# Six norms of an encoder trunk: the spread of rsqrt by a DRAM round trip in place of diagonals and a matmul with ones

## The chip, the cores and the metric

The kernel runs on one NeuronCore of one Trainium2 chip. The core has a tensor engine (PE, with its weight loads shown apart as PEld), a vector engine (DVE), a scalar engine (ACT), GpSimd (POOL) and SyncE (SP), which issues most of the DMA transfers. Each engine works through its own instructions in the order in which they were laid down, and waits on semaphores for the others. The metric is the device time of one execution in microseconds, and less is better.

## The reference

The model is a trunk of two layers over 1024 tokens of width 1024. Layer 0 mixes tokens with grouped-query attention, layer 1 with a chunked gMLP; both are followed by a squared-ReLU MLP. Ahead of each of these four stages stands an RMS norm that is modulated by the conditioning vector:

```python
def rmsnorm(x, g):
    xf = x.astype(jnp.float32)
    y = xf * lax.rsqrt(jnp.mean(xf * xf, axis=-1, keepdims=True) + EPS)
    return (y * g).astype(x.dtype)
...
        h = modulate(rmsnorm(x, norm1_g[i]), sh1, sc1)
...
            y = gqa_attention(h, w_qkv[j], q_g[j], k_g[j], w_o[j], cos, sin)   # layer 0
            y = chunked_gmlp(h, w_in[j], b_in[j], ...)                         # layer 1
        x = x + g1[:, None, :] * y
        h = modulate(rmsnorm(x, norm2_g[i]), sh2, sc2)
        x = x + g2[:, None, :] * sq_relu_mlp(h, mlp_w_in[i], mlp_w_out[i])
```

Everything is float32. Four norms, each over two halves of the tokens, make eight norms in the kernel.

## The kernel before

**Layout.** The activations lie transposed: the 1024 features are 8 tiles of 128 partitions, and the 1024 tokens are two halves of 512 columns. A tile `x[hf][k]` is 128 x 512. A float32 product is made of three matmuls: each operand is split into a high part (a cast on ACT, L328 in `split`) and a low part (a subtraction, L329, on DVE as a rule).

**The products.** The large products follow a Winograd/Strassen scheme with seven products ("1265473") of combinations of quarter operands. One step of it, here called a unit, is 12 matmuls of 128 x 512. `winograd` (L469 to L471 are its matmuls) makes the first product of the two MLPs and a part of gMLP's; `wino_v` makes gMLP's other part; `Out` (L1212 to L1214) makes the products that come back to width 1024. Each of these calls a hook after a unit, with the unit's number, and the hook traces the work of the next norm between the products.

**The norm.** `SquareSum` adds up the squares of 8 tiles as they become final. `norm_ss` then sums over the 128 partitions with four small matmuls against a column of ones (L274), which leaves the mean square of token p + 128 j at partition p and column j. DVE adds EPS and scales (L276), and POOL raises this to the power of -0.5 (L242, in `rsqrt_small`), which gives `r`, 128 x 4. But the activations need it with tokens along the columns and the same value on all partitions. So ACT makes four diagonals, the identity times a column of r (L284; L280 does it in one DVE instruction for the first two norms), and `norm_rb` multiplies them by a matrix of ones (L289): every partition of the 128 x 512 result holds the 512 values. The result is read from PSUM (`keep`) or copied to SBUF by ACT first (L293).

**Its use.** `norm_h` multiplies a tile by rb (L334) and applies scale and shift (L335). `forms_a` makes the eight such tiles of half 0 and splits them, one tile a step; `more` takes steps from its list. `forms_b` makes the eight tiles of half 1 and the combinations "6", "5", "4", "7", "3" that the scheme needs (L376, L377, L388); its list has four steps for the tiles with "6", then one for each other combination. The first units use half 0 alone: with FIRST = 6 the MLPs' first twelve units are "1" and "2", and "6" is first wanted by unit 12; `wino_v` wants it at unit 8.

**The places.** Two norms (layer 0, ahead of attention) are not touched. The other six, numbered as they come:

1. Layer 0, second norm, half 0: in the loop over the output projection (L1425 to L1431). `norm_ss` after block m = 0, `norm_rb` and the first steps after m = 1. A block is 24 matmuls.
2. Layer 0, second norm, half 1: in `mlp`'s hook `at`, at unit HB[0] = 2; `norm_rb` and `forms_b` at HB + HR = 4, then one step a unit.
3. Layer 1, first norm, half 0: `norm_hook`, called over the last 32 units of MLP 0's output; `norm_ss` at m = HK = 3, `norm_rb` at m = 5, then a step at every odd m.
4. Layer 1, first norm, half 1: in `gmlp`'s hook, at unit HBV = 1; `norm_rb` at 3, then steps at 4 to 7, 10, 12, 16 and 20.
5. Layer 1, second norm, half 0: `norm_hook` again, over the last 24 units of gMLP's output.
6. Layer 1, second norm, half 1: as number 2, with HB[1] = 1 and HR[1] = 1, so at unit 1 and unit 2.

**Order.** The code is traced as written, and a scheduler lays the instructions of each engine in an order of its own: among those that are ready by its own estimate of time, the one that was traced first goes first. `pin` keeps an instruction behind the one traced before it on its engine; `hold` does so in the first stage alone. Tiles come from pools: `slot()` takes one of 58 SBUF tiles "t" of 128 x 512, `bank_x` and `bank_y` one of four PSUM banks each. The `dram` pool holds what is kept in DRAM between stages.

Of the kernel before, what the change touches and what calls it, by code (L numbers as in the profile page):

```python
# [11 lines left out]
F32 = mybir.dt.float32  # L12
F32R = mybir.dt.float32r
AF = mybir.ActivationFunctionType
ALU = mybir.AluOpType
# [3 lines left out]
P = 128  # L19
D = 1024  # L20
# [16 lines left out]
def encoder_kernel(ctx: ExitStack, tc: tile.TileContext, t: dict, out: bass.AP):  # L37
# [3 lines left out]
    const = ctx.enter_context(tc.tile_pool(name="const", bufs=1))  # L41
    small = ctx.enter_context(tc.tile_pool(name="small", bufs=3))
    mem = ctx.enter_context(tc.tile_pool(name="mem", bufs=1))

    uid = [0]

    def nm(s):
        uid[0] += 1
        return f"{s}_{uid[0]}"
# [220 lines left out]
    def norm_ss(sqs, bank, wide_dg=False):  # L270
        acc = sqs.acc
        ps = bank("ss")[:, :4]
        for j in range(4):
            hold(T.matmul(ps[:, j : j + 1], acc[:, j * P : (j + 1) * P], ones[:, 0:1], start=True, stop=True))  # L274
        ms = small.tile([P, 4], F32, tag="ms", name=nm("ms"))
        hold(V.tensor_scalar(ms, ps, 1.0 / D, EPS, ALU.mult, ALU.add))  # L276
        r = rsqrt_small(ms, 4)
        dg = slot()
        if wide_dg:
            hold(V.tensor_tensor(dg.rearrange("p (j q) -> p j q", j=4), ident.unsqueeze(1).broadcast_to([P, 4, P]),  # L280
                                 r.unsqueeze(2).broadcast_to([P, 4, P]), ALU.mult))
            return dg
        for j in range(4):
            S.activation(dg[:, j * P : (j + 1) * P], ident, AF.Copy, scale=r[:, j : j + 1])  # L284
        return dg

    def norm_rb(dg, bank, keep=False):
        ps = bank("rb")
        hold(T.matmul(ps, ones, dg, start=True, stop=True))  # L289
        if keep:  # L290
            return ps
        rb = slot()
        S.copy(rb, ps)  # L293
        return rb

    def norm_u(xk, layer, which, k, rb):
# [42 lines left out]
    def forms_a(xt, layer, which, rb):  # L339

        f = {"raw": {}}

        def step(k):
            if k < KT:
                f["raw"][k] = norm_h(xt[k], layer, which, k, rb, G if k in NA else V)
            if k:
                f[("1" if k < 5 else "2", (k - 1) % 4)] = split(f["raw"][k - 1])

        f["todo"] = [lambda k=k: step(k) for k in range(KT + 1)]
        return f  # L350
# [742 lines left out]

    es_a.close()
    p_y = ctx.enter_context(tc.tile_pool(name="p_y", bufs=4, space=PSUM))
    dram = ctx.enter_context(tc.tile_pool(name="dram", bufs=1, space=bass.MemoryType.DRAM))

    class Out:


# [239 lines left out]
    def mlp(layer, fs, sqs, done, hook):  # L1340
        hidden = forms_dram(16)
        out_ = Out(t["wm"][layer], hidden, 4, mod[:, layer, 5])
        quad = {}
        f = {}
        stores = []

        def sink(c, m, hf):
            S.activation(c, c, AF.Relu)
            S.activation(c, c, AF.Square)
            p = m // 2  # L1350
            quad[(m, hf)] = c
            q = early((m % 2, hf))
            if q:
                nc.scalar.dma_start(hidden[p][q], c)
                if q == "1" and p < FIRST:
                    del quad[(m, hf)]
                elif q == "2" and p < FIRST:
                    quad[(m - 1, 0)] = slot()
                    nc.sync.dma_start(quad[(m - 1, 0)], hidden[p]["1"])
            else:  # L1360
                tiles = {(j, h): quad.pop((m + j, h)) for j in range(2) for h in range(2)}
                stores.extend(spread(tiles, hidden[p], slot, V))

        n = 16 * 7
        rest = []
        halves = None if layer else Halves(late)

        def at(i):
            more(f, RW, None)
            if halves:  # L1370
                h = i - 13
                if 0 <= h < 2 * KT:
                    spill(h // KT, (h % KT,))
                elif h == 2 * KT:
                    halves.start()
                elif h == 2 * KT + 4:
                    halves.silu()
                    halves.load()
                    halves.load()
                elif h > 2 * KT + 6 and h % MX == 0:  # L1380
                    halves.step()
            if i == HB[layer]:
                rest.append(norm_ss(sqs[0], bank_y))
            elif i == HB[layer] + HR[layer]:
                rest[:] = forms_b(f, x[1], layer, 1, norm_rb(rest[0], bank_y, True), "5473")
            elif i > HB[layer] + HR[layer] and rest:
                rest.pop(0)()
            if stores and i % 7 > 0 and i % 7 != 6:
                stores.pop(0)()
            out_.ahead(i - n)  # L1390

        yield from winograd(lambda m: t["wi"][layer, m], 16, f, sink, FIRST, at, lambda: (cut(8), f.update(fs[0])))

        def at_out(i):
            if stores and i > 2:
                stores.pop(0)()
            if i == CUT:
                cut(4)
            if halves and i in XL:
                load_xs(*XL[i])  # L1400
            if hook and i >= out_.n - out_.tail:
                hook(i - out_.n + out_.tail)

        if halves:
            load_xs(*XL[-1])
        out_.run(at_out, done)
# [13 lines left out]
    for m in range(WA):  # L1420
        if m == WA - 1:
            mlp0_fs, mlp0_sqs = [None], [sqB]
            mlp0.append(mlp(0, mlp0_fs, mlp0_sqs, lambda *a: add_sq(*a), lambda i: hook0(i)))
            next(mlp0[0])
        wo_mm(m, (1,), bank_y)  # L1425
        if m == 0:
            fA = norm_ss(sqA, bank_x)
        elif m == 1:
            fA = forms_a(x[0], 0, 1, norm_rb(fA, bank_x))
        if m:  # L1430
            more(fA, RQ, None)  # L1431
    cond.clear()

# [6 lines left out]
    def norm_hook(layer, which, bank):  # L1440
        dg = []

        def hook(m):
            if m == HK:
                dg.append(norm_ss(sq[0], bank))
                sq[0] = SquareSum()
            elif m == HK + 2:
                fg.append(forms_a(x[0], layer, which, norm_rb(dg[0], bank)))
                more(fg[-1], 1, None)
            elif m > HK + 2:  # L1450
                more(fg[-1], m % 2, None)
        return hook

# [156 lines left out]
    def gmlp(f, sqB, done, hook):  # L1610
        rest = []

        def at(i):
            more(f, RW, None)
            if i == HBV:
                spill(0)
                rest.append(norm_ss(sqB, bank_y))
            elif i == HBV + 2:
                rest[:] = forms_b(f, x[1], 1, 0, norm_rb(rest[0], bank_y), "5734", True)
            elif rest and i in (*range(HBV + 3, HBV + 7), 10, 12, 16, 20):  # L1620
                rest.pop(0)()
                if len(rest) == 4:
                    spill(1)
# [147 lines left out]
HK = 3  # L1771
# [79 lines left out]
```

## Time and profile before

| | us |
|---|---|
| Median of the runs shown (3) | 2627.94 |
| Lowest and highest of them | 2626.04, 2629.11 |
| Profiled execution, span from first to last instruction | 2625.8 |

The profile gives no time of that execution beside its span; the median of the runs lies 2.1 us above it.

| Engine | busy us | share of the span | instructions |
|---|---|---|---|
| PE | 2601.6 | 99% | 12860 |
| DVE | 2183.1 | 83% | 3276 |
| ACT | 1451.1 | 55% | 2612 |
| POOL | 723.2 | 28% | 531 |

The profile is of one execution. A row of a group gives the line, the engine, the operation, output and inputs by the program's names, the shapes and the count, then busy time and the mean duration in ns, then the idle time of the engine ahead of it and what ended that. A row of a timeline gives start and duration in us, the engine, the line, and in brackets the idle time before and what ended it. A row of a window gives its length, then busy time and count for PE, PEld, DVE, ACT and POOL, the granted PE clock, the DMA engines' busy share and GB/s. Matmuls are pipelined: a duration of 0.39 us overlaps the next one, and the distance between starts is what a matmul costs. Tiles are named by their pool's tag, so many tiles are called t.

### The profile page before, as it was taken

How to read it: one execution, taken by the hardware profiler on the slowest of the kernel's cores; microseconds unless marked ns; L12 is line 12 of the kernel's file. 1: busy time of each engine (PE TensorE's matmuls, PEld its weight loads, DVE VectorE, ACT ScalarE, POOL GpSimd, SP SyncE). 2: the span in 40 equal slices, each digit the busy share in tenths (PEclk: the TensorE clock that was granted, in tenths of full speed). 3: DMA queues.
4: the chain of work that ended last, by engine and by line, in shares of the span. 5: the costliest groups of instructions: out<-in, count | busy, mean ns of one | idle time of the engine just before them, and what ended most of it. 6: DMA issues, size and time to landing. Idle time of an engine off the chain costs nothing. (4 is left out here: it accounts for less than half of the span.)

```text
span 2625.8 us, 37307 instructions
## 1 busy us (share of the span) xinstructions
PE 2601.6 (99%) x12860; PEld 2172.2 (83%) x12860; DVE 2183.1 (83%) x3276; ACT 1451.1 (55%) x2612; POOL 723.2 (28%) x531
## 2 busy tenths in 40 slices
PE   9999999999999999999999999999999999999999
PEld 7789999888788888888888888888888788888887
DVE  7868999887989989877897687788979977789974
ACT  4569999854654455446543354445456645465442
POOL 0238776533000004430122054451520000005400
PEclk9999999999999999999999999999999999999999
DMA  8010222234486788545243355568641554487461
GB/s 306 27 33 9 74 88 75 97 112 145 168 288 245 270 310 306 192 133 172 82 136 121 120 174 175 178 204 305 237 141 50 177 179 156 153 310 268 149 211 58
DMA packets 208752, 435.39 MB, mean 166 GB/s; under 512 B 23025, under 2 KB 35441, under 8 KB 208562
## 3 DMA queue, kind: packets, MB, share of 16 engines
q1 hardware_dynamic: 181682, 395.24, 44.7%
q10 hardware_dynamic: 26880, 37.76, 4.0%
q8 instruction: 102, 1.67, 0.3%
q14 instruction: 88, 0.72, 0.1%
HBM read 310.23 MB, written 122.68 MB: 165 GB/s over the span
## 5 line engine op out<-in xcount | busy, mean ns | idle before, releaser
L1212 PE MATMUL out<-t,s 128*128 128x512 f32 x1232 | 479.9, 390 | 0.9 <-ACT t L328 0.8
L1213 PE MATMUL out<-t,s 128*128 128x512 f32 x1232 | 479.3, 389 | 0.7 <-DVE t L329 0.7
L1214 PE MATMUL out<-t,s 128*128 128x512 f32 x1232 | 478.9, 389 | 0.0
L469 PE MATMUL w<-t,s 128*128 128x512 f32 x1168 | 459.8, 395 | 0.9 <-ACT t L328 0.5
L470 PE MATMUL w<-t,s 128*128 128x512 f32 x1168 | 455.2, 390 | 1.8 <-DVE t L329 1.8
L471 PE MATMUL w<-t,s 128*128 128x512 f32 x1168 | 454.7, 389 | 0.0
L329 DVE TENSOR_TENSOR t<-t,t 128x512 fp32r<-128x512 f32 x408 | 324.7, 806 | 36.2 <-ACT t L328 29.0
L328 ACT CAST t<-t 128x512 fp32r<-128x512 f32 x408 | 245.3, 617 | 122.2 <-DMA t<-hf 71.7
L1213 PEld LDWEIGHTS out<-t,s 128*128 128x128 f32 x1232 | 231.2, 188 | 50.2 <-DVE t L329 1.8
L1212 PEld LDWEIGHTS out<-t,s 128*128 128x128 f32 x1232 | 231.2, 188 | 50.2 <-ACT t L328 1.7
L1214 PEld LDWEIGHTS out<-t,s 128*128 128x128 f32 x1232 | 231.2, 188 | 48.1
L454 ACT CAST s<-w 128x512 fp32r<-128x512 f32 x292 | 173.4, 616 | 161.4 <-PE w L471 104.3
L470 PEld LDWEIGHTS w<-t,s 128*128 128x128 f32 x1168 | 219.3, 188 | 49.7 <-DVE t L329 5.2
L469 PEld LDWEIGHTS w<-t,s 128*128 128x128 f32 x1168 | 219.3, 188 | 49.4 <-issue 2.9
L471 PEld LDWEIGHTS w<-t,s 128*128 128x128 f32 x1168 | 219.2, 188 | 45.6
L455 DVE TENSOR_TENSOR s<-w,s 128x512 fp32r<-128x512 f32 x292 | 221.8, 766 | 41.1 <-ACT s L454 40.6
L1194 ACT CAST s<-t 128x512 fp32r<-128x512 f32 x240 | 148.2, 620 | 187.0 <-PE out L1214 136.3
L1180 POOL TENSOR_TENSOR w<-w,t 128x512 f32<-128x512 f32 x20 | 34.2, 1721 | 767.7 <-DMA t<-hf 691.5
L1195 DVE TENSOR_TENSOR s<-t,s 128x512 fp32r<-128x512 f32 x240 | 195.1, 814 | 56.1 <-ACT s L1194 55.4
L951 DVE TENSOR_REDUCE mx<-s 128x1 f32<-128x1024 f32 x128 | 156.2, 1220 | 30.5 <-PE s L948 29.2
L974 DVE TENSOR_TENSOR t<-t,t 128x512 fp32r<-128x512 f32 x256 | 164.1, 681 | 17.1 <-ACT t L968 16.4
L984 PE MATMUL o<-t,t 128*128 128x256 f32 x1024 | 162.6, 291 | 0.0
(251 smaller groups left out, 5089.1 us busy)
## 6 DMA issues: line engine op xcount, KB each, us to landing
t<-hf SPq DMA_DIRECT2D x320, 256.0 KB, 4.0
hf<-c SPq DMA_DIRECT2D x156, 256.0 KB, 3.4
w<-in_wi_dram SPq DMA_DIRECT2D x64, 512.0 KB, 4.5
hf<-c ACTq DMA_DIRECT2D x96, 256.0 KB, 2.7
w<-in_ada_dram SPq DMA_DIRECT2D x36, 512.0 KB, 3.9
x<-in_ada_dram SPq DMA_DIRECT2D x64, 256.0 KB, 5.4
t<-in_wm_dram SPq DMA_DIRECT2D x64, 256.0 KB, 4.7
wf<-w SPq DMA_DIRECT2D x64, 256.0 KB, 3.0
```

Of the source, the lines that this page charges most:

```text
L328: S.copy(hi, src)
L329: (eng or V).tensor_tensor(lo, src, f32(hi), ALU.subtract)
L454: S.copy(hi, src)
L455: V.tensor_tensor(lo, src, f32(hi), ALU.subtract)
L469: T.matmul(ps, hi[:, a], th, start=kt == 0, stop=False)
L470: T.matmul(ps, hi[:, a], tl, start=False, stop=False)
L471: T.matmul(ps, lo[:, a], th, start=False, stop=kt == 3)
L974: pin(V.tensor_tensor(lo, pt, f32(hi), ALU.subtract))
L1195: V.tensor_tensor(lo, src, f32(hi), ALU.subtract)
L1212: T.matmul(ps, hi[:, a], th, start=begin and kt == 0, stop=False, **g)
L1213: T.matmul(ps, hi[:, a], tl, start=False, stop=False, **g)
L1214: T.matmul(ps, lo[:, a], th, start=False, stop=end and kt == 3, **g)
```

## The change

A new function `norm_bc` takes the place of `norm_ss` and `norm_rb` at the six places. The partition sums, the scaling and the power stay. Then `r` (128 x 4) is stored to a 4 x 128 tile in DRAM, so that the 512 values lie in the order of the tokens, and this row is loaded into all 128 partitions of an SBUF tile. Both transfers are issued by SP. The first multiplication by rb is traced three units after `norm_bc` in the hooks of half 1 (before: two, one and two units after, at places 2, 6 and 4), four units after it in `norm_hook` (before: two), and two blocks after it in the output projection (before: one). The lists of steps follow from there. The DRAM pool is opened at the start.

```diff
+    dram = ctx.enter_context(tc.tile_pool(name="dram", bufs=1, space=bass.MemoryType.DRAM))
...
+    def norm_bc(sqs, bank):
+        acc = sqs.acc
+        ps = bank("ss")[:, :4]
+        for j in range(4):
+            T.matmul(ps[:, j : j + 1], acc[:, j * P : (j + 1) * P], ones[:, 0:1], start=True, stop=True)
+        ms = small.tile([P, 4], F32, tag="ms", name=nm("ms"))
+        V.tensor_scalar(ms, ps, 1.0 / D, EPS, ALU.mult, ALU.add)
+        r = rsqrt_small(ms, 4)
+        d = dram.tile([4, P], F32, name=nm("rd"))
+        nc.sync.dma_start(d.rearrange("j p -> p j"), r)
+        rb = slot()
+        nc.sync.dma_start(rb, d.rearrange("j p -> (j p)").unsqueeze(0).broadcast_to([P, 512]))
         return rb
...
             if i == HB[layer]:
-                rest.append(norm_ss(sqs[0], bank_y))
-            elif i == HB[layer] + HR[layer]:
-                rest[:] = forms_b(f, x[1], layer, 1, norm_rb(rest[0], bank_y, True), "5473")
-            elif i > HB[layer] + HR[layer] and rest:
+                rest.append(norm_bc(sqs[0], bank_y))
+            elif i == HB[layer] + 3:
+                rest[:] = forms_b(f, x[1], layer, 1, rest[0], "5473")
+            elif i > HB[layer] + 3 and rest:
                 rest.pop(0)()
...
         if m == 0:
-            fA = norm_ss(sqA, bank_x)
-        elif m == 1:
-            fA = forms_a(x[0], 0, 1, norm_rb(fA, bank_x))
-        if m:
+            fA = norm_bc(sqA, bank_x)
+        elif m == 2:
+            fA = forms_a(x[0], 0, 1, fA)
+        if m > 1:
             more(fA, RQ, None)
...
             if m == HK:
-                dg.append(norm_ss(sq[0], bank))
+                dg.append(norm_bc(sq[0], bank))
                 sq[0] = SquareSum()
-            elif m == HK + 2:
-                fg.append(forms_a(x[0], layer, which, norm_rb(dg[0], bank)))
+            elif m == HK + 4:
+                fg.append(forms_a(x[0], layer, which, dg[0]))
                 more(fg[-1], 1, None)
-            elif m > HK + 2:
+            elif m > HK + 4:
                 more(fg[-1], m % 2, None)
...
-                rest.append(norm_ss(sqB, bank_y))
-            elif i == HBV + 2:
-                rest[:] = forms_b(f, x[1], 1, 0, norm_rb(rest[0], bank_y), "5734", True)
-            elif rest and i in (*range(HBV + 3, HBV + 7), 10, 12, 16, 20):
+                rest.append(norm_bc(sqB, bank_y))
+            elif i == HBV + 3:
+                rest[:] = forms_b(f, x[1], 1, 0, rest[0], "5734", True)
+            elif rest and i in (*range(HBV + 4, HBV + 8), 10, 12, 16, 20):
                 rest.pop(0)()
```

More of the change, by code (lines that the diff above doesn't have):

```diff
@@ L293, in norm_rb @@
         S.copy(rb, ps)
+        return rb
+    def norm_bc(sqs, bank):
[10 more added lines that the diff above has]
+        nc.sync.dma_start(rb, d.rearrange("j p -> (j p)").unsqueeze(0).broadcast_to([P, 512]))
         return rb
```

1 line of the change is left out of this document (removed).

## The prediction

> **What bounds the kernel now.** I read the page first (span, busy shares), then the groups by line for what is removed, then windows, waits and timelines around the six places.
>
> ```profile
> span 2625.8 us, 37307 instructions
> PE 2601.6 (99%) x12860; PEld 2172.2 (83%) x12860; DVE 2183.1 (83%) x3276; ACT 1451.1 (55%) x2612; POOL 723.2 (28%) x531
> L289 PE MATMUL rb<-t,ones 128*128 128x512 f32 x16 | 8.4, 606 | 1.0 <-DVE t L280 0.9 <-ACT t L284 0.2
> ```
>
> PE is busy 99% of the span: what is taken from PE's stream comes off the time, if PE isn't made to wait instead. The third row is the matmul with ones: 8 norms, each in two passes (x16), 8.4 us in all. Six of the eight go. I number them: 1 is the half 0 norm inside the output projection, 2 the half 1 norm at the start of MLP 0, 3 the half 0 norm in the tail of MLP 0's output, 4 the half 1 norm in gMLP's first product, 5 the half 0 norm in the tail of gMLP's output, 6 the half 1 norm at the start of MLP 1.
>
> What one matmul really costs is read from the starts on PE around it (number 3; the columns are start, duration, engine):
>
> ```profile
> 1190.01 0.39 PE L1214 MATMUL out<-t,s 128*128 128x512 f32 x1
> 1190.24 1.02 PE L289 MATMUL rb<-t,ones 128*128 128x512 f32 x2
> 1190.70 0.80 PE L1212 MATMUL out<-t,s 128*128 128x512 f32 x1
> 1191.34 0.40 PE L1213 MATMUL out<-t,s 128*128 128x512 f32 x1
> 1191.57 0.40 PE L1214 MATMUL out<-t,s 128*128 128x512 f32 x1
> ```
>
> The product's matmuls start 0.23 us apart (1191.34 to 1191.57). From 1190.01 the third one after would start at 1190.70 without L289; it starts at 1191.57: 0.87 us.
>
> But PE doesn't set the pace everywhere. At 2 and 6 the half 1 forms are made by VectorE in a rush, and PE waits for them (windows: length, then busy time of PE, PEld, DVE, ACT, POOL; then PE's waits in 640 to 700 and 2008 to 2060):
>
> ```profile
> 626.00:655.00 29.00, 29.00 (x131) 23.59 (x131) 28.87 (x39) 19.20 (x32) 7.44 (x3) 1.00 0.32 109
> 655.60:658.70 3.10, 2.93 (x14) 1.96 (x12) 0.16 (x2) 1.91 (x6) 1.01 (x1) 1.00 0.00 0
> 659.00:691.00 32.00, 29.68 (x120) 21.45 (x118) 31.74 (x54) 24.99 (x44) 0.00 (x0) 1.00 0.29 99
> 2019.00:2046.00 27.00, 25.23 (x108) 19.58 (x106) 26.93 (x46) 21.07 (x36) 0.00 (x0) 1.00 0.20 68
> PE w L470 <- DVE t L329: 1.8, 6, 0.5
> PE w L469 <- ACT t L328: 1.2, 1, 1.2
> ```
>
> DVE is busy 31.74 of 32 us and 26.93 of 27 us behind the two norms, PE only 29.68 and 25.23. So there the end is set by when DVE gets the spread rsqrt, plus a fixed amount of DVE work. Just ahead of 2 DVE has a hole (0.16 of 3.10 us busy): it waits for the norm. There the change is decided.
>
> **Removed.** 24 diagonals on ACT, six matmuls, four copies of rb on ACT (2 and 6 read it from PSUM). ACT is busy 55% of the span, so its share costs nothing by itself. The chain at 2:
>
> ```profile
> 655.75 1.01 POOL L242 TENSOR_TENSOR r<-ms,mhalf 128x4 f32<-128x4 f32 x1 [19.06 <-DVE ms L276]
> 656.79 1.28 ACT L284 ACTIVATE t<-ident,r 128x128 f32<-128x128 f32 x4 [2.62 <-POOL r L242]
> 657.57 0.39 PE L471 MATMUL w<-t,t 128*128 128x512 f32 x1
> 658.12 1.12 PE L289 MATMUL rb<-t,ones 128*128 128x512 f32 x2 [0.17 <-ACT t L284]
> 658.61 0.69 DVE L329 TENSOR_TENSOR t<-t,t 128x512 fp32r<-128x512 f32 x1 [2.94 <-ACT t L328]
> 659.28 0.69 DVE L334 TENSOR_TENSOR t<-x,rb 128x512 f32<-128x512 f32 x1
> 659.31 0.40 PE L470 MATMUL w<-t,t 128*128 128x512 f32 x1
> ```
>
> The diagonals stand at the head of ACT's queue for 2.62 us until POOL has r; a split (L328) waits behind them, and DVE's L329 behind that. This block goes, so DVE does that 0.6 us of work inside the hole. PE loses 659.31 - 657.57 - 2 x 0.23 = 1.28 us here, and about 0.9 us at each other place.
>
> I call c the time from r's end to the first multiply with rb (L334). The starts of L242 and L334 at the other five, in the order 1, 3, 4, 5, 6:
>
> ```profile
> 616.29 1.48 POOL L242 TENSOR_TENSOR r<-ms,mhalf 128x4 f32<-128x4 f32 x1
> 623.19 1.28 DVE L334 TENSOR_TENSOR t<-x,t 128x512 f32<-128x512 f32 x2
> 1185.07 1.44 POOL L242 TENSOR_TENSOR r<-ms,mhalf 128x4 f32<-128x4 f32 x1 [7.28 <-DVE ms L276]
> 1191.92 0.69 DVE L334 TENSOR_TENSOR t<-x,t 128x512 f32<-128x512 f32 x1
> 1269.01 1.40 POOL L242 TENSOR_TENSOR r<-ms,mhalf 128x4 f32<-128x4 f32 x1 [4.73 <-DVE ms L276]
> 1275.97 1.28 DVE L334 TENSOR_TENSOR t<-x,t 128x512 f32<-128x512 f32 x2
> 1951.58 1.43 POOL L242 TENSOR_TENSOR r<-ms,mhalf 128x4 f32<-128x4 f32 x1 [7.27 <-DVE ms L276]
> 1958.42 0.69 DVE L334 TENSOR_TENSOR t<-x,t 128x512 f32<-128x512 f32 x1
> 2014.28 1.01 POOL L242 TENSOR_TENSOR r<-ms,mhalf 128x4 f32<-128x4 f32 x1 [27.64 <-DVE ms L276]
> 2019.08 0.68 DVE L334 TENSOR_TENSOR t<-x,rb 128x512 f32<-128x512 f32 x1
> ```
>
> So c is now 5.4 at 1, 2.5 at 2 (659.28 - 656.76), 5.4 at 3, 5.6 at 4, 5.4 at 5 and 3.8 at 6.
>
> **Added.** Two transfers in a row on SP: r's 512 elements as runs of 4 bytes, then the 2 KB row read 128 times. No such store is in the trace. The nearest rows (issues: KB each, median us to landing) and, last, the spread of vd's landings:
>
> ```profile
> vd<-x ACTq DMA_DIRECT2D x48, 256.0 KB, 2.4
> xd<-x SPq DMA_DIRECT2D x32, 256.0 KB, 4.5
> t<-in_wi_dram SPq DMA_DIRECT2D x16, 256.0 KB, 3.0
> x<-in_bv_dram SPq DMA_DIRECT2D x6, 256.0 KB, 4.9
> DMA to landing us min/median/max: 2.1/2.4/5.4
> ```
>
> For the store: 2.1 us is the shortest of the stores with the shortest runs (vd, 1 KB), 4.5 us the median of stores made in a crowd (xd). For the load: 3.0 us is that of the equal-sized in_wi loads, 4.9 us that of in_bv, which is also one row to 128 partitions. I take 2.2 and 3.0, because SP issues nothing from 641.7 (640.37 + 1.28) to 677.57 and from 2008.1 to 2036.89 (rows below), where it matters; with 0.1 us for the hand-over, c is 5.3 us. Its ends are 5.1 (2.1 + 3.0) and 9.4 (4.5 + 4.9).
>
> ```profile
> 640.37 1.28 SPq L422 DMA_DIRECT2D t<-in_wi_dram  x3
> 677.57 7.54 SPq L416 DMA_DIRECT2D w<-in_wi_dram  x2
> 2005.54 2.59 SPq L422 DMA_DIRECT2D t<-in_wi_dram  x2
> 2036.89 6.94 SPq L416 DMA_DIRECT2D w<-in_wi_dram  x2
> ```
>
> The Trainium skill, "DMA: Bandwidth & Descriptors", section "Anatomy of one DMA", gives, for transfers prepared in software, a fixed 2.0 us (mostly the receipt of the last write) plus the bytes over 436 GB/s; the shortest store here, 2.1 us, is near that. My estimate from it for both transfers is 2.0 + 2.6 = 4.6 us, and the sum below would be 1.4 us lower.
>
> The new wait: the load waits on SP for its own store, some 2 us, and SP's later issues stand behind it. At 2 and 6 nothing is due on SP (rows above). At 3 and 5 they are loads of forms, traced eight units of 2.7 us before use; I cost that at nothing. Without that cover it would be the store's 2.2 us at each, 4.4 us in all. At 2 and 6 rb now holds an SBUF slot where it held a PSUM bank: between nothing and one more wait for a slot, which I put in the range.
>
> **Moved.** The forms are traced one unit later at 2 and 4, two later at 3, 5 and 6, one projection block later at 1. At 3 and 5 the last step falls eight units before, or on, the last unit of the tail; its splits are first used six units (16 us) into the next product, so it costs nothing; used at once, it would cost the two units, 5.4 us. At 2, 4 and 6 the fourth step is still traced three units ahead of its first use. I expect DVE to take a form as soon as rb is there.
>
> **The sum.** Against the 2625.8 us span:
> - 2: h starts 5.3 - 2.5 = 2.8 us later, DVE has no slack behind it: +2.8. The 1.28 us of PE are eaten, since PE only waits longer for DVE.
> - 6: 5.3 - 3.8 = +1.5, by the same argument.
> - 1 and 4: c is as before (5.4, 5.6); DVE is full behind 1 (28.87 of 29.00) and the matmul's gain goes into later waits: 0.
> - 3 and 5: c as before, PE sets the pace: -0.9 each, -1.8.
>
> In all +2.5: a span of 2628.3. The median of the runs shown, 2627.94, lies 2.1 above the span, so 2630.4, rounded to **2630 us**.
>
> **Rivals.**
> (a) *Faster: the hole is filled.* DVE finds other ready splits while it waits, helped by ACT's freed queue, and the forms have slack. For it: ACT's 2.62 us block at 2 goes, and at 6 the forms were traced two units earlier than they now need be. Against it: DVE sat idle in the hole, with little ready. Then all six matmuls count: 5 x 0.88 + 1.28 = 5.7 us less, 2622 us.
> (b) *Slower: the store's small runs.* If a 4-byte run is costly to write, c is long. Above 5.5 us, 1 and 4 are late too and the sum is (c - 2.5) + (c - 3.8) + (c - 5.4) + (c - 5.6) - 1.8. It passes +5.3 us (0.2%) at c = 6.1, so 0.8 us over my estimate decides; at c = 7.5 it is +10.9, 2639 us; at 9.4, 2646 us. For it: no run in the trace is so short, and in_bv's broadcast took 4.9. Against it: quiet queues at 2 and 6. The Trainium skill speaks for it on the same page: "Specifications" puts full rate at 512 B and up, with a read-modify-write below, and "Rules for kernel authors" warns that a strided last dimension becomes one descriptor per element. No run here shows it.
> (c) *Half filled:* DVE hides half of the 2.8 and 1.5 us, so 2 and 6 cost 2.1 us, 3 and 5 give 1.8, and the time is 2628 us. For it: L329 at 2 can now go before rb; against it: that is 0.6 us of work, not 1.4.
>
> **How the numbers follow.** About 0.2%, 5.3 us, is what a measurement of this kernel tells from no change. The forecast has 0.37 and (c) 0.20; both are within 0.2%, 0.57 together, with a range of their own of 2623 to 2633. Rival (a) has 0.13, (b) 0.30, most of it below 2639. The range 2622 to 2639 leaves out some 0.15 to 0.2: beyond (a), and c over 7.5.
>
> **What would show it.** In the new trace: six fewer L289 pairs, four L289 records left; the r store landing 2 to 2.5 us after its issue and the load some 3 us later; DVE's hole at 2 and 6 grown to 5 or 6 us; PE's waits for L329 and L328 behind them grown by 2 to 3 us and 1 to 2 us; starts at 3 and 5 without the 0.87 us step. I am wrong if the store lands after 4 us or more, if DVE does other work in the hole, if DVE's order puts other work in front of forms whose rb is there, or if loads behind SP's wait starve PE in the two tails.

## The result and the profile after

The changed kernel takes 2674.77 us (median of 4 runs, 2673.00 to 2675.54) against 2628.53 us of the kernel before on the same chip: a ratio of 1.0182, 95% interval 1.0170 to 1.0194, or 46.2 us more. The profiled execution took 2673.0 us, its span is 2671.2. The prediction, 2630 us with a range to 2639, was far too low. One of the five executions of p4, a run below, was slow at 6513.28 us and is left out of its median.

The first lines of the page after are the span and the busy time of each engine. In the table of groups the matmul with ones has the row below them.

```profile
span 2671.2 us, 37288 instructions
...
PE 2616.0 (98%) x12848; PEld 2174.5 (81%) x12848; DVE 2182.3 (82%) x3276; ACT 1442.0 (54%) x2584; POOL 721.0 (27%) x531
...
L290 PE MATMUL rb<-t,ones 128*128 128x512 f32 x4 | 2.1, 618 | 0.7 <-DVE t L281 0.7
```

The work went as the diff says: 12 matmul instructions of the six norms are gone (x16 to x4), and DVE's work is the same to 1 us. PE's busy time nevertheless grew from 2601.6 to 2616.0 us with fewer matmuls, so some matmuls ran slower, and the rest of the 45 us is waiting. The two new transfers, seen by their lines (store L306, load L308; the last row of each gives the time from issue to landing):

```profile
L306 SPq DMA_DIRECT2D rd<-r x6: 371/376/388, 616.5 to 2049.6; - x6
...
DMA to landing us min/median/max: 7.7/7.9/8.8
```

```profile
L308 SPq EVENT_SEMAPHORE  x6: 17/7576/8357, 624.2 to 2050.0; - x6
L308 SPq DMA_DIRECT2D t<-rd x6: 319/323/333, 624.3 to 2057.7; - x6
...
DMA to landing us min/median/max: 4.4/5.7/6.1
```

The store lands after 7.9 us, not 2.2, and the load after 5.7, not 3.0. SP meanwhile stands at the load's wait (the EVENT_SEMAPHORE row: up to 8.4 us). What follows at place 2 is in the timeline after (start, duration, engine; in brackets the idle time before and what ended it):

```profile
659.29 1.40 POOL L243 TENSOR_TENSOR r<-ms,mhalf 128x4 f32<-128x4 f32 x1 [25.28 <-DVE ms L303]
...
660.72 0.38 SPq L306 DMA_DIRECT2D rd<-r  x1
...
668.57 0.33 SPq L308 DMA_DIRECT2D t<-rd  x1
668.99 2.08 SPq L437 DMA_DIRECT2D t<-in_wi_dram  x3
674.87 0.62 ACT L343 CAST t<-t 128x512 fp32r<-128x512 f32 x1 [9.64 <-DMA t<-in_wi_dram]
...
675.52 0.69 DVE L344 TENSOR_TENSOR t<-t,t 128x512 fp32r<-128x512 f32 x1 [11.77 <-ACT t L343]
676.13 2.49 DVE L349 TENSOR_TENSOR t<-x,t 128x512 f32<-128x512 f32 x4
```

DVE, which paces this stretch, is idle for 11.77 us. Two waits end almost together. The spread row lands at 674.2 (668.57 + 5.7, the median). And the weight loads L437, issued at 640.37 in the kernel before, ahead of the norm, now stand on SP behind the load's wait and go out at 668.99; a cast on ACT needs them, and DVE needs the cast. c, from r's end (660.69) to the first multiply (L349 at 676.13), is 15.4 us, where the prediction had 5.3 and an upper end of 9.4.

PE's waits over the whole span (total, times, longest), and windows (length, busy PE, PEld, DVE, ACT, POOL, then the granted clock):

```profile
PE w L484 <- ACT t L343: 13.2, 8, 3.3
PE v L1582 <- ACT t L343: 6.1, 3, 3.5
PE out L1225 <- ACT t L343: 4.4, 3, 2.8
```

```profile
650.00:660.00 10.00, 6.89 (x25) 5.25 (x26) 8.23 (x16) 5.35 (x11) 0.71 (x1) 0.66 0.00 0
...
680.00:690.00 10.00, 6.90 (x16) 4.32 (x17) 10.00 (x17) 7.64 (x14) 0.00 (x0) 0.66 0.30 105
```

The same windows of the kernel before:

```profile
650.00:660.00 10.00, 9.83 (x45) 7.38 (x44) 7.02 (x14) 6.92 (x16) 1.01 (x1) 1.00 0.00 0
...
680.00:690.00 10.00, 7.70 (x27) 4.05 (x25) 9.78 (x17) 8.53 (x16) 0.00 (x0) 1.00 0.52 173
```

The clock falls behind PE's waits and makes part of the loss. The starts of the same instructions of DVE and ACT that read or feed the products, set side by side in the two traces, show where the 46 us arise: 17 us by the end of place 2, 3 at place 3, 8 at 4, 6 at 5 and 12 at 6. Hardly any of it is gained back later.

### The profile page after: what moved, and what is told of

It reads as the page before. It is cut to its first block, busy times and chain, and to the rows that moved or that the text cites. A ratio compares the mean times of both kernels' runs of the same rounds, so it can differ in the third digit from the quotient of the medians.

```text
span 2671.2 us, 37288 instructions
## 1 busy us (share of the span) xinstructions
PE 2616.0 (98%) x12848; PEld 2174.5 (81%) x12848; DVE 2182.3 (82%) x3276; ACT 1442.0 (54%) x2584; POOL 721.0 (27%) x531
## 4 chain that ended last, share of the span: by engine, by line
PE 86%; DVE 7%; DMA 3%; ACT 3%; issue 1%; POOL 0%; SPq 0%; DVEq 0%; ACTq 0%
PE w L484 10%; PE out L1226 10%; PE w L485 10%; PE out L1227 10%; PE out L1225 10%; PE w L486 10%; PE s L963 4%; PE o L999 4%; PE t L980 3%; PE v L1582 3%; PE v L1583 3%; PE v L1584 3%; PE mix L1674 2%; DVE t L344 1%; PE qkv L590 1%
## 5 line engine op out<-in xcount | busy, mean ns | idle before, releaser
L989 DVE TENSOR_TENSOR t<-t,t 128x512 fp32r<-128x512 f32 x256 | 164.2, 682 | 16.9 <-ACT t L983 16.1
```

## The experiments

All medians and ratios at a glance; each ratio is to the kernel before, run on the same chip.

| run | median us | ratio, 95% interval |
|---|---|---|
| p1: place 1 alone | 2636.50 | 1.0038 (1.0024 to 1.0052) |
| p26: places 2 and 6 alone | 2655.91 | 1.0113 (1.0097 to 1.0130) |
| p35: places 3 and 5 alone | 2636.77 | 1.0039 (1.0024 to 1.0054) |
| p4: place 4 alone | 2636.07 | 1.0033 (1.0019 to 1.0047) |
| poolq: transfers on POOL's queue | 2672.25 | 1.0177 (1.0161 to 1.0192) |
| moved: matmul kept, all at the later steps | 2653.84 | 1.0109 (1.0092 to 1.0126) |
| forms_late: matmul as before, forms later | 2635.39 | 1.0037 (1.0024 to 1.0050) |
| run512: store in runs of 512 B | 2640.81 | 1.0054 (1.0039 to 1.0069) |
| early512: the same, forms at the old steps | 2639.65 | 1.0050 (1.0035 to 1.0065) |
| run16: store in runs of 16 B | 2636.83 | 1.0044 (1.0030 to 1.0057) |
| early16: the same, everything computed, old steps | 2655.56 | 1.0108 (1.0094 to 1.0122) |
| freerb: load waits for no store | 2626.05 | 0.9997 (0.9988 to 1.0006) |
| rnow: no spreading at all | 2617.97 | 0.9971 (0.9961 to 0.9982) |
| pooldg: diagonals on POOL | 2625.57 | 0.9997 (0.9988 to 1.0006) |
| stores_a, stores_b, strides: added stores (single runs) | 2625.02, 2627.12, 2630.54 | not compared |

### Which places lose: one part of the change alone

Each of these kernels is the kernel before with the change at the named places only. p26:

```diff
@@ mlp, hook at (places 2 and 6); nothing else changes
-                rest.append(norm_ss(sqs[0], bank_y))
-            elif i == HB[layer] + HR[layer]:
-                rest[:] = forms_b(f, x[1], layer, 1, norm_rb(rest[0], bank_y, True), "5473")
-            elif i > HB[layer] + HR[layer] and rest:
+                rest.append(norm_bc(sqs[0], bank_y))
+            elif i == HB[layer] + 3:
+                rest[:] = forms_b(f, x[1], layer, 1, rest[0], "5473")
+            elif i > HB[layer] + 3 and rest:
```

p35 does it in `norm_hook`, p4 in gMLP's hook and p1 in the loop over the output projection, each with its own hunk of the change.

> The change at places 2 and 6 alone. Late-rb theory: c goes from 2.5 and 3.8 to about 13.5 us, and DVE has no slack, so 10 to 20 us come on top: 2637 to 2648 us. Queue theory: nothing else is due on SP, at most +4 us, 2631 us.

> The change at places 3 and 5 alone (tails of the two output products). Round-trip theory (rb is late, DVE-bound stretches suffer): these two are not DVE-bound, so at most +2 us (2627 to 2631 us). Queue theory (the load's wait holds up SP, and the loads behind it come late): +7 to +10 us (2635 to 2639 us), with the loads of forms behind the wait seen late.

> The change at place 4 alone. Late-rb theory: c goes from 5.6 to about 14 us with DVE full behind it, +7 to +11 us: 2634 to 2638 us. With place 1 as the remainder of the 46 us. If it costs less than 4 us, the loss seen there in the full change came from what happened ahead of it.

> The change at place 1 alone. The changes at 3 and 5, at 2 and 6 and at 4 alone cost 9.7, 29.0 and 9.7 us, 48.4 in all, against 46 to 47.8 for the whole. If the places add up, place 1 alone is at -2 to +2 us: 2625 to 2630. If its late forms keep PE waiting in the first product as they do where only the tracing is moved (8 us there), it is 2633 to 2640 and the sum of the parts exceeds the whole, because the delay of place 2 covers that of place 1.

p26 costs 29.0 us, p4 9.1, p1 9.2 and p35 9.7. The timeline of p26 at both places:

```profile
654.28 1.01 POOL L243 TENSOR_TENSOR r<-ms,mhalf 128x4 f32<-128x4 f32 x1 [19.05 <-DVE ms L303]
...
666.47 0.34 SPq L308 DMA_DIRECT2D t<-rd  x1
666.86 1.37 SPq L437 DMA_DIRECT2D t<-in_wi_dram  x3
671.47 0.62 ACT L343 CAST t<-t 128x512 fp32r<-128x512 f32 x1 [14.35 <-DMA t<-in_wi_dram]
672.12 0.69 DVE L344 TENSOR_TENSOR t<-t,t 128x512 fp32r<-128x512 f32 x1 [16.47 <-ACT t L343]
672.73 2.49 DVE L349 TENSOR_TENSOR t<-x,t 128x512 f32<-128x512 f32 x4
...
2027.99 1.01 POOL L243 TENSOR_TENSOR r<-ms,mhalf 128x4 f32<-128x4 f32 x1 [27.69 <-DVE ms L303]
...
2045.92 1.29 DVE L349 TENSOR_TENSOR t<-x,t 128x512 f32<-128x512 f32 x2
```

c is 17.4 us at 2 (672.73 - 655.29) and 16.9 at 6 (2045.92 - 2029.00). By the prediction's rule, c less the old c, that is 14.9 + 13.1 = 28.0 us; measured are 29.0. For p1 the rows of r and of the first multiply are these (at p4's place r ends at 1268.92 and the multiply starts at 1282.38):

```profile
617.31 1.48 POOL L243 TENSOR_TENSOR r<-ms,mhalf 128x4 f32<-128x4 f32 x1
...
632.33 2.84 DVE L349 TENSOR_TENSOR t<-x,t 128x512 f32<-128x512 f32 x1 [4.76 <-DMA t<-rd]
```

c is 13.5 us at both; less 5.4 and 5.6 this is 8.1 and 7.9, and 9.2 and 9.1 were measured. So the rule holds to within 2 us at four places, with c measured and not guessed. It fails at 3 and 5, where it gave -1.8 and 9.7 came out. The timeline of p35 at place 3 shows one way in which the time is lost:

```profile
1185.69 0.38 SPq L306 DMA_DIRECT2D rd<-r  x1
1194.26 0.33 SPq L308 DMA_DIRECT2D t<-rd  x1
1194.68 0.38 SPq L1175 DMA_DIRECT2D t<-wf  x1
...
1201.10 0.62 ACT L1207 CAST s<-t 128x512 fp32r<-128x512 f32 x1 [9.84 <-DMA t<-wf]
...
1201.75 0.69 DVE L1208 TENSOR_TENSOR s<-t,s 128x512 fp32r<-128x512 f32 x1 [9.61 <-ACT s L1207]
```

SP is held from 1185.69 to 1194.26, and the loads of weight and activation forms for the product under way stand behind it. When the first of them lands, ACT has been idle for 9.84 us and DVE for 9.61; PE, which waited for nothing there in the kernel before (1205 to 1250), then waits 2.2 us for DVE's splits and 1.5 for ACT's.

The four parts add up to 57.0 us, the whole costs 46.2. Places 1 and 2 alone bring 11 and 14 us by the starts of these instructions, together only 17: most of the difference is there. That the wait at place 2 runs partly in the shadow of that at place 1 is argued, not shown.

### Is SP's held queue enough? poolq

```diff
-        nc.sync.dma_start(d.rearrange("j p -> p j"), r)
+        nc.gpsimd.dma_start(d.rearrange("j p -> p j"), r)
...
-        nc.sync.dma_start(rb, d.rearrange("j p -> (j p)").unsqueeze(0).broadcast_to([P, 512]))
+        nc.gpsimd.dma_start(rb, d.rearrange("j p -> (j p)").unsqueeze(0).broadcast_to([P, 512]))
```

> As the changed kernel, but store and load are issued from POOL, so that nothing else on SP waits. Queue theory: most of the 46 us goes, below 2645 us. Round-trip theory: rb is as late as before, the stretches behind 1, 2, 4 and 6 lose the same, 2660 to 2675 us, and only the 9 us of 3 and 5 go.

The time stays at 2672.25 us. The timeline of poolq at place 2:

```profile
661.86 0.83 POOL L306 DMA_DIRECT2D rd<-r  x1 [0.29 <-POOL r L243]
...
671.24 0.56 POOL L308 DMA_DIRECT2D t<-rd  x1 [8.56 <-DMA rd<-r]
...
675.41 2.50 DVE L349 TENSOR_TENSOR t<-x,t 128x512 f32<-128x512 f32 x4 [8.08 <-DMA t<-rd]
```

The first multiply with the row at places 3 and 5 of the same run:

```profile
1218.46 0.69 DVE L349 TENSOR_TENSOR t<-x,t 128x512 f32<-128x512 f32 x1 [7.23 <-DMA t<-rd]
...
2001.95 0.69 DVE L349 TENSOR_TENSOR t<-x,t 128x512 f32<-128x512 f32 x1 [11.12 <-DMA t<-rd]
```

SP is free now, and at place 2 DVE no longer waits for a cast but for the spread row itself, and resumes as late. Of two waits that end together, taking one away brings nothing. The same holds at 3 and 5, where a gain of 9 us was expected: DVE waits 7.23 and 11.12 us for the row, with the splits for the product behind that multiply in its queue. By the starts of the same matmuls on PE, set side by side, places 3 and 5 lose 3.4 and 6.9 us here against 3.4 and 6.7 in the changed kernel. So p35 shows a held queue that suffices for this loss, and poolq a late row that suffices without it. What the held queue would cost with the row in time, no run shows.

### Is it the later tracing? moved and forms_late

moved has the diagonals and the matmul, at the changed kernel's later steps; forms_late has the matmul at the old steps and only the forms later. For place 1:

```diff
 # moved
-            fA = norm_bc(sqA, bank_x)
+            fA = norm_ss(sqA, bank_x)
         elif m == 2:
-            fA = forms_a(x[0], 0, 1, fA)
+            fA = forms_a(x[0], 0, 1, norm_rb(fA, bank_x))
 # forms_late
-            fA = norm_bc(sqA, bank_x)
+            fA = norm_ss(sqA, bank_x)
+        elif m == 1:
+            fA = norm_rb(fA, bank_x)
         elif m == 2:
             fA = forms_a(x[0], 0, 1, fA)
```

> Diagonals and matmul with ones as before at all six places; only the later tracing of the forms is kept. Round-trip theory and queue theory: within 4 us of the kernel before (2624 to 2633 us). Theory that the later tracing itself costs the time: 2645 us or more.

> Diagonals and matmul with ones at their old steps (at 2 and 6 copied to SBUF too), so rb is there when it was before; the forms alone are traced at the changed kernel's later steps. Theory that the later tracing costs the time, because DVE and ACT put other work in front: 2638 to 2655 us, about as the kernel in which both were moved (2653.8). Theory that only a late rb costs: 2624 to 2631 us.

moved loses 26.7 us: a matmul traced later is also done later on PE, so c grows with it, which makes this run no clean test of the steps. It is one of the prediction's rule, with no transfer in the way: c is 10.9, 7.5, 17.0 and 7.9 us at places 1, 2, 4 and 6, and less the old c that is 5.4 + 5.0 + 11.4 + 4.2 = 26.0 us. At 3 and 5 its c is 10.9 as well, and by the starts on PE nothing is lost there.

forms_late loses 8.4 us, between the two expectations. By the starts on PE, some 6 us of it arise at place 1, where rb is as early as before (4.7 us behind r's end), and 3 at place 2, where the copy of rb to SBUF ends 5.4 us behind r's end and the multiply used to start at 2.5. PE's timeline at place 1 (rows with a wait), and a window:

```profile
649.82 0.50 PE L484 MATMUL w<-t,t 128*128 128x512 f32 x1 [2.38 <-ACT t L343]
652.41 0.79 PE L486 MATMUL w<-t,t 128*128 128x512 f32 x1 [1.86 <-DVE t L344]
```

```profile
650.00:660.00 10.00, 8.14 (x29) 6.39 (x30) 6.74 (x12) 3.53 (x8) 1.40 (x1) 0.66 0.00 0
```

The half 0 forms come behind other work in the queues of DVE and ACT, PE waits for their splits in MLP 0's first units, and the clock falls. So the later step costs some 6 us by itself at place 1, even with rb on time. At place 2 the run can't tell the step from the later rb, and elsewhere it costs next to nothing.

### Is it the 4-byte runs? run512, early512, run16, early16

run512 stores a tile of 128 x 128 with r in its first four columns, so that each partition writes 512 bytes; the loaded values are not the norms'. early512 is the same with the forms traced at the old steps.

```diff
-        r = rsqrt_small(ms, 4)
-        d = dram.tile([4, P], F32, name=nm("rd"))
-        nc.sync.dma_start(d.rearrange("j p -> p j"), r)
+        r = padr
+        G.tensor_tensor(r[:, :4], ms, mhalf.broadcast_to([P, 4]), ALU.pow)
+        d = dram.tile([P, P], F32, name=nm("rd"))
+        nc.sync.dma_start(d, r)
```

> As the changed kernel, but r stands in a 128 x 128 tile that is stored whole in runs of 512 B; the load reads one 2 KB row of it, so the norms get wrong values. If the 4-byte runs are what makes the store take 7.8 us, it lands in 2 to 2.5 us, the round trip falls from 13.5 to about 8 us and the time to 2636 to 2650 us (round-trip and queue theory alike). If the store is slow because a dependent load follows it, or for its place, it stays at 7 us or more and the time near 2675 us.

> The kernel with the 512 B runs (2640.8 us, wrong values in the norms), but with the forms traced at the old, earlier steps. Tracing theory: the 13.7 us left there go, 2624 to 2632 us. Late-rb theory: the load's 3 to 4.6 us and the store's 2 us are what is left, 2637 to 2643 us as before.

run16 stores r as it lies, 16 bytes a partition; the load then spreads the rsqrts in another order of the tokens.

```diff
-        d = dram.tile([4, P], F32, name=nm("rd"))
-        nc.sync.dma_start(d.rearrange("j p -> p j"), r)
+        d = dram.tile([P, 4], F32, name=nm("rd"))
+        nc.sync.dma_start(d, r)
```

> The changed kernel with r stored as it lies, 128 runs of 16 bytes in place of 512 of 4; the rsqrts then reach the wrong tokens. If the store's time goes with the number of runs (512 runs 7.9 us, 1 run per partition of 512 B 1.5 to 2.2 us), it lands after 2 to 3.5 us and the time is near that with 512 B runs: 2640 to 2648 us. If it is the length of a run below 512 B that costs, each write being a read and a write of its surroundings, it lands after 6 us or more and the time stays at 2660 to 2675.

These three lose 13.7, 12.7 and 9.5 us to the kernel before, where the whole change loses 46.2. run16's stores and loads:

```profile
L306 SPq DMA_DIRECT2D rd<-r x6: 319/323/331, 616.4 to 2020.9; - x6
...
DMA to landing us min/median/max: 1.4/1.4/2.0
```

```profile
L308 SPq DMA_DIRECT2D t<-rd x6: 319/323/327, 618.5 to 2022.4; - x6
...
DMA to landing us min/median/max: 3.0/5.0/5.5
```

So some three quarters of the loss is the form of the store, and it is not shortness as such: runs of 16 bytes land in 1.4 us like those of 512. What is left, 9.5 us in run16, fits the prediction's sum: with this run's c of 8.7, 8.4, 9.6, 5.7, 9.4 and 8.6 us in the order of the places it is 3.3 + 5.9 + 0.1 + 4.8 - 1.8 = 12.3, and the interval allows 7.9 to 15. The load, with the store at its best ahead of it, puts the row 5.3 to 7.5 us behind r's end in these three runs: far later than the matmul at 2 and 6 (2.5 and 3.8 us), and no earlier than it by over 0.2 us anywhere. In early512 DVE waits 6.35 us for it at place 2 and 4.07 at 6, and at place 1 c is as before.

The sum does not fit early512. With its c of 5.4, 6.1, 6.4 and 7.5 us at places 1, 2, 4 and 6 it gives 0 + 3.6 + 0.8 + 3.7 - 1.8 = 6.3 us, and 12.7 were measured, with an interval of 9.2 to 17.1. By the starts on PE some 9 us of it arise at place 2, where the granted clock is 0.83 from 670 to 690 us. So for a short c the rule gives too little there, and the rest is not explained. That the earlier forms would win back run512's 13.7 us is refuted.

early16 is the change with that store made whole: the multiply reads the spread row in the order of the tokens, and the forms are at the old steps.

```diff
+        return rb.rearrange("q (p j) -> q j p", j=4)
...
+            eng.tensor_tensor(u.rearrange("q (j p) -> q j p", j=4), xk.rearrange("q (j p) -> q j p", j=4), rb, ALU.mult)
```

> The change with r stored as it lies (128 runs of 16 bytes), the multiply reading the spread row in the order of the tokens, and the forms traced at the steps of the kernel before; everything is computed. Store 1.4 to 2 and load 3 to 5.5 us make a c of 5 to 7.5 us. By the prediction's own sum with that c, (c - 2.5) + (c - 3.8) + what c has over 5.4 and 5.6 at 1 and 4 - 1.8, it is 2630 to 2638 us. If the late tracing was most of what run16 lost, 2628 to 2631; if the strided read slows the multiply, above 2640.

At 2655.56 us it is worse than run16 and far above the 2630 to 2638 of the sum. Its multiply, by the groups of DVE (busy us, mean ns, idle before):

```profile
L350 DVE TENSOR_TENSOR t<-x,t 128x512 f32<-128x512 f32 x45 | 49.4, 1128 | 14.0 <-DMA t<-rd 14.0
```

The strided read makes 44 of the 45 multiplies 1.05 to 1.12 us long, against 0.68 to 0.69, on the engine that paces places 2 and 6, and DVE waits 14.0 us for the row besides. early512 has the same steps, and DVE waits 14.1 us for the row there, but its 45 multiplies take 31.7 us in place of 49.4. It loses 12.7 us and early16 28.8, so some 16 us go to the strided read.

### Why is the store slow? stores_a, stores_b, strides

These are the kernel before with one added store of r at each place, which nothing waits for; six shapes in two orders, then 128 runs of 4 bytes at six distances.

```diff
 # stores_a and stores_b: one of these at each place
+    nc.sync.dma_start(dram.tile([4, P], F32, name=nm("rd")).rearrange("j p -> p j"), r)
+    nc.sync.dma_start(dram.tile([P, 4, 16], F32, name=nm("rd"))[:, :, 0:1], r.unsqueeze(2))
...
 # strides: n = 16, 2, 8, 4, 1, 32 at places 1 to 6
+    nc.sync.dma_start(dram.tile([P, n], F32, name=nm("rd"))[:, 0:1], r[:, 0:1])
```

> The kernel before with one added store of r at each of the six places, each of another shape, which nothing waits for; the norms are spread as before. In the order of the places 1 to 6: 512 runs of 4 bytes side by side (as in the change), 128 runs of 16 bytes, 512 runs of 4 bytes 64 bytes apart, 256 runs of 8 bytes, 512 runs of 4 bytes 512 bytes apart, 128 runs of 4 bytes. If the number of runs sets the time: 7 to 9 us for all three with 512 runs, 2.5 to 5 for 256, 1.4 to 2 for both with 128. If it is the size of 4 bytes: 128 runs of 4 bytes also take 5 us or more. If it is neighbouring runs that different DMA engines write into the same stretch of DRAM: the stores 64 and 512 bytes apart land in 1.5 to 3 us. The time itself should stay within 0.2% of before, as nothing waits.

> As the run with six stores of r, the shapes moved on by three places: 256 runs of 8 bytes at place 1, 512 runs of 4 bytes 512 bytes apart at 2, 128 runs of 4 bytes at 3, 512 runs of 4 bytes side by side at 4, 128 runs of 16 bytes at 5, 512 runs of 4 bytes 64 bytes apart at 6. Each theory expects of each shape what it expects there; if the place rather than the shape sets the time, the times stay with the places.

> The kernel before with one added store at each of the six places that nothing waits for: 128 runs of 4 bytes (one column of r), in the order of the places 1 to 6 at a distance of 64, 8, 32, 16, 4 and 128 bytes. So far: 512 and 128 runs at 4 bytes' distance 7.7 to 9.7 us, 512 runs at 64 and 512 bytes' distance 2.3 to 3.2. If writes into one stretch of 64 bytes follow each other at some 0.5 us each (16 of them 8 us), the store lands after about 1.5 us at 64 and 128 bytes, 2 at 32, 2.5 at 16, 4 to 5 at 8 and 8 to 10 at 4. If only runs that touch one another are slow, 8 bytes and more all give 1.5 to 3 us. If 128 runs of 4 bytes are slow in themselves, all six take over 5 us.

| shape of the store | landing us |
|---|---|
| 512 runs of 4 B, side by side (the change) | 8.5 and 8.1 |
| 512 runs of 4 B, 64 B apart | 2.9 and 3.2 |
| 512 runs of 4 B, 512 B apart | 2.3 and 2.5 |
| 256 runs of 8 B, side by side | 3.0 and 3.6 |
| 128 runs of 16 B, side by side | 1.4 and 3.1 |
| 128 runs of 4 B, side by side | 9.7, 9.2 and 8.5 |
| 128 runs of 4 B, 8 B apart | 5.1 |
| 128 runs of 4 B, 16, 32, 64, 128 B apart | 1.5, 1.4, 2.1, 1.4 |

Three rows of stores_a's trace, the change's own shape (L285), the same 512 runs 64 bytes apart (L287), and 128 runs side by side (L296):

```profile
L285 SPq DMA_DIRECT2D rd<-r x1: 381/381/381, 616.4 to 616.4; - x1
DMA to landing us min/median/max: 8.5/8.5/8.5
...
L287 SPq DMA_DIRECT2D rd<-r x1: 599/599/599, 1185.2 to 1185.2; - x1
DMA to landing us min/median/max: 2.9/2.9/2.9
...
L296 SPq DMA_DIRECT2D rd<-r x1: 326/326/326, 2012.0 to 2012.0; - x1
DMA to landing us min/median/max: 9.7/9.7/9.7
```

The number of runs doesn't set the time: 128 side by side take longer than 512 that are apart. Nor does the size of 4 bytes. It is 4-byte runs packed into the same stretch: at 8 bytes' distance the store is still slow (5.1, one store), which speaks against "only runs that touch", and at 16 bytes' it is quick. A time per write into a stretch of 64 bytes fits only in its direction: at 8 and 16 bytes' distance it forecast 4 to 5 and 2.5, measured are 5.1 and 1.5, and 256 runs of 8 bytes, which also put eight writes into 64 bytes, land in 3.0 to 3.6. In all the slow stores, runs that are neighbours in DRAM come from different partitions; 4-byte runs side by side from one partition were not tried. Why such stores are slow stays open.

### What would the removal be worth? freerb, rnow, pooldg

In freerb the load reads numbers of the input `cond` and so waits for no store; in rnow nothing is spread at all, and the multiply takes one column of r. In both the norms get other factors, and the forms are at the old steps.

```diff
 # freerb
-        nc.sync.dma_start(rb, d.rearrange("j p -> (j p)").unsqueeze(0).broadcast_to([P, 512]))
+        nc.sync.dma_start(rb, t["cond"][:, :512].broadcast_to([P, 512]))
 # rnow: in place of store and load
+        return r[:, 0:1].broadcast_to([P, 512])
```

> The changed kernel, but the broadcast load reads 512 numbers of the input cond, so that it waits for no store, and the forms are traced at the steps of the kernel before. The store of r is kept, nothing waits for it, and the spread values are not the norms'. So the diagonals, the matmuls and the copies are gone and rb is early at all six places. If the six matmuls are worth PE's 5.7 us of rival (a) once rb is no longer late, the time is 2621 to 2624 us (before 2627 to 2628.5). If DVE sets the pace at the places anyhow, it is 2625 to 2629. If the two added transfers cost time even when nobody waits for them (SP's queue, DMA traffic), it is above 2630.

> The changed kernel with the forms traced at the steps of the kernel before, and without store, load, diagonals and matmul: VectorE multiplies by one column of r, read again along the row, so that all norms get the rsqrt of the wrong token. c is then 0 to 0.5 us everywhere: no spreading can be faster. If PE's time is what counts once rb is not late, rival (a)'s 5.7 us are gained and more: 2619 to 2623 us. If DVE and the order of the work set the pace around the places, earlier forms bring little: 2624 to 2627, and the removed matmuls were never worth their 5.7 us.

freerb shows no difference from before; at place 1 its load took 9 us, so that DVE still waited 6.39 us for it, and the run couldn't settle the question. That its slow stores, kept but waited for by nobody, cost little is not shown by freerb, where gains and losses may cancel; it is made likely by the single runs stores_a and stores_b, which lie within the 2623.83 to 2629.36 us of the kernel before on their chip. rnow is 8.8 us faster by the medians, 4.7 to 10.2 by the interval. Its timeline at place 2:

```profile
653.95 1.01 POOL L243 TENSOR_TENSOR r<-ms,mhalf 128x4 f32<-128x4 f32 x1 [20.74 <-DVE ms L303]
654.99 2.50 DVE L345 TENSOR_TENSOR t<-x,r 128x512 f32<-128x512 f32 x4 [1.12 <-POOL r L243]
```

With c = 0 the prediction's sum gives -2.5 at 2, -3.8 at 6 and -1.8 at 3 and 5, so -8.1, and up to -9.9 if PE's 0.9 us count at 1 and 4 too. Measured is -8.8, so the prediction's rule holds on this side too. By it, 6.3 us are the earlier row at 2 and 6 and only 1.8 the removed matmuls; the run can't tell that split from rival (a)'s 5.7 us for the matmuls with a smaller gain by the row. Either way a gain is there, and it is lost where the row comes later than the matmul's.

pooldg was a try to gain something of this with everything computed: the kernel before with the four diagonals made by one POOL instruction.

```diff
+        if not pinned[0]:
+            G.tensor_tensor(dg.rearrange("p (j q) -> p j q", j=4), ident.unsqueeze(1).broadcast_to([P, 4, P]),
+                            r.unsqueeze(2).broadcast_to([P, 4, P]), ALU.mult)
+            return dg
```

> The kernel before, with the four diagonals of each of the six norms made by one POOL instruction instead of four ACT instructions; the matmul with ones stays. It takes ACT's block behind r away and puts no transfer in its place. POOL is idle 72% of the span. If the block on ACT is what delays VectorE's splits at place 2, 1 to 3 us are gained: 2624 to 2627. If POOL's instruction on 128 x 512 elements takes longer than the four of ACT (1.28 us), c grows by 1 to 2 us at each place and the time is 2629 to 2636.

Its 2625.57 us can't be told from before. No version that computes everything beat the kernel before.

## Why the prediction was wrong

- **The bound: right.** That places 2 and 6 are paced by DVE, with the end set by when it gets the row, is what p26 shows (28.0 us by the rule, 29.0 measured), moved without any transfer (26.0 and 26.7), and rnow from the other side. For early512 the rule gives too little (6.3 against 12.7), which stays open.
- **"I take 2.2 and 3.0 ... c is 5.3 us": wrong, and this is the step that failed.** The store's price came from stores with runs of 1 KB; 7.7 to 8.8 us were measured (median 7.9), and 4.4 to 6.1 for the load (5.7). The store is the larger part: with 16-byte runs the loss falls from 46.2 to 9.5 us (run16). The bounds of 2.1 to 4.5 did not hold it either, because they came from rows of another form, and the one thing that was new in this store, 4-byte runs side by side, had no row. Rival (b) named this mechanism and its chance was 0.30, but its price stopped at 9.4, where c came out at 12.7 to 16.9.
- **"At 3 and 5 ... I cost that at nothing" and "c as before": wrong.** SP's hold was 8.6 us, not 2.2, and c in the changed kernel is 16.7 and 16.9 us, where it was 5.4; 9.7 us were lost where 1.8 were to be gained (p35). The held queue suffices for that loss, and so does the late row at the head of DVE's queue (poolq). The price without cover, 4.4 us, was in the text but not in a rival.
- **"At 2 and 6 nothing is due on SP": wrong.** SP issued nothing there because the weight loads L422 (L437 after) had been issued at 640.37, ahead of the norm. In the new order they stand behind its load. A gap in a queue says what was issued in the old order, not what a new wait will stand in front of. It cost nothing of its own, since the row was as late (poolq).
- **"I expect DVE to take a form as soon as rb is there": wrong at place 1.** With rb on time, the later step alone cost some 6 us there (forms_late).
- **The clock: not foreseen.** PE's waits of some 3 us are followed by the windows at a granted clock of 0.66 shown above. The Trainium skill, "TensorE: Matmul & The Clock Gate", section "Why this matters for your kernels", asks for no gaps of more than about 3 us between bursts of matmuls, since a window of idling brings the clock back to half. The waits of 3.3 and 3.5 us and the fall of the clock agree with it; but in forms_late two waits of 2.38 and 1.86 us, close together, went with the same 0.66, so one gap of that length isn't needed. The mean granted clock went from 0.999 to 0.993 of full speed, which over the span of 2671.2 us is some 16 us of clock: at most that much of the loss, and less where DVE was the bound anyhow.

Put together: with the measured c (13.5 at 1, 15.4 at 2, 12.7 at 4, 16.0 at 6) the prediction's rule gives 8.1 + 12.9 + 7.1 + 12.2 = 40.3 us, and p35's 9.7 for places 3 and 5 makes 50.0; 46.2 were measured. That places 1 and 2 partly cover each other is argued above, not shown.

Rival (b) drew on the Trainium skill's "DMA: Bandwidth & Descriptors", section "Specifications", by which full rate needs 512 B and a shorter transfer becomes a read-modify-write. That is a rule on rate, and it doesn't give the landing of these small stores: runs of 16 bytes land in 1.4 us (median of run16; one of stores_b took 3.1), runs of 512 in 1.5, and it is 4-byte runs at a distance under 16 bytes that cost.

## What to carry to other kernels

A transfer whose form has no row in the profile (the size of its runs and how densely they lie where they are written) should be priced by a run of that form beside the kernel, which costs one store that nobody waits for; bounds from rows of another form don't hold. A load that waits for its own store makes its whole queue wait, so list what that queue will issue next in the new order, not in the old one. And a DRAM round trip pays only where the value isn't wanted yet: by the prediction's sum, an estimate, it had to be no longer than some 4 us here (c - 2.5 + c - 3.8 - 1.8 = 0 at c = 4.05), and the shortest store and load in a row that the runs show took 5.2.

## What the runs showed of the hardware

- 128 numbers of 4 bytes stored side by side take 8.5 to 9.7 us to land, with 8 bytes between their starts 5.1 (one store), and 1.4 to 2.1 with 16 bytes or more. 512 of them behave alike: 7.7 to 8.8 in the changed kernel (up to 11.7 in freerb), 2.3 to 3.2 when 64 bytes or more apart.
- One 2 KB row read to 128 partitions took 3.0 to 6.3 us in most of these runs, 9.2 at worst (freerb), with a median of 5.7 in the changed kernel and 5.0 in run16.
- DVE multiplies 128 x 512 float32 in 0.69 us, and in 1.05 to 1.12 us where one operand is read with a stride of 16 bytes (early16); a column read again along the row (rnow) costs nothing extra, 2.50 us for four.
